# Laying small vectors, the router and the spatial weights out by channel on the host, in a hybrid decoder trunk

## The chip, the cores and the metric

The kernel runs on one core of a Trainium2 chip. The metric is the device time of one execution in microseconds; the host's preparation of the inputs is not in it. A core has a matrix engine (TensorE, PE in the profile), a vector engine (VectorE, DVE), an activation engine (ScalarE, ACT), a general one (GpSimd, POOL) and an engine that mostly issues transfers (SyncE, SP). Data lie in SBUF (128 partitions) and in PSUM, where the matmuls write. SP and ACT each issue transfers on a queue of their own: q1 (SP) and q10 (ACT) in the profile.

## The reference

x is 256 tokens by 1024 channels in float32. There are two layers, each a mixer and a feed-forward block, and a final RMS norm. What the change touches is in the mixer:

```
h = RMSNorm(x; norm_mix);  a, gate, u, v = split(h @ W_in, 4)       # 512 columns each
c = a * sigmoid(gate)
c = silu(group_norm(causal_depthwise_conv(c, conv_w, width 31) + conv_b; conv_ng, conv_nb))
u = gelu(u);  v = head_norm(gelu(v); sgu_ng, sgu_nb)                # 4 heads of 128 columns
ws = tril(sgu_w)                                                    # 4 heads, 128 x 128
g = u * (ws @ v + sgu_b)                                            # per chunk of 128 tokens
x = x + concat(c, g) @ W_out
x = x + FFN(RMSNorm(x; norm_ffn))       # layer 0: dense SwiGLU; layer 1: top 2 of 8 experts
```

## The kernel before

The program runs mixer 0, the dense block, mixer 1, the experts and the final norm one after the other, with one stream of weights under all of them. The weights lie in DRAM as blocks of up to 1 MB; `load_raw` (L325 to L344) issues one on SP into one of 11 raw buffers (`wraw`). A unit of 128 x 1024 is split for the exact three-pass float32 matmul: its high part `whi` by ACT (L353), its low part `wlo` by DVE or POOL (L358). A buffer comes free when its splits are done, or, where the weights are used unsplit, its matmuls.

A mixer (`mixer`, L557) is written as a list of operations for a small scheduler. Each operation is added by `add(engine, cost, function, reads, writes, delay)`; the scheduler sorts the whole list by modelled costs, by the length of the path behind an operation and by the delay after which its result counts as ready (2.0 us for SP's small loads, 4.0 for ACT's), and issues the program in that order. Each engine then runs its own instructions in that order, and an instruction that waits holds up all that are behind it on its engine.

In mixer 0, x comes in two halves (`xs`). ACT squares it (L706) for the RMS norm and, with DVE, makes the two parts `xh` (L699) and `xl` (L701) of each 128 channels out of PE's transposes (L686), scaled with a gain from `vt`. The conv gate and value (`gate`, `a`) come out of PSUM through DVE (L808, L812), which multiplies them by the token's 1/rms; the GLU product is L818, and the depthwise conv is one DVE instruction per tap (L863, L865), some taps on POOL (L842) and PE (L854). u and v are projected next; v's statistics are L933 to L935, its normalisation L941 on ACT, its gain and offset (`sgb`) L947 on DVE and POOL, the product with the spatial weights (`wst`) L954 on PE, and the gate L958. The output projection is L997.

The small inputs: `vt` (128 x 64) holds the per-channel vectors, a column each for 128 channels, and `cwt` (128 x 2 x 124) the conv taps. Both are made on the chip. Seven small loads bring rows (`rowa`, `crow`, `rowb`), PE transposes them (L744, L762, L764), and DVE and ACT copy them out (L745, L766, L768). `wst` is loaded by ACT with `sgu_w` as it is, four rows of 512 bytes for each partition (L771), transposed by PE (L927) and multiplied by the triangle `trim` out of PSUM (L929). `sgb` is two loads on ACT's queue (L774) that put one row of 2 KB into each of 128 partitions. The router (`rw`) is loaded in the dense block.

Of the kernel before, what the change touches and what calls it, by code (L numbers as in the profile page):

```python
# [7 lines left out]
F32 = mybir.dt.float32  # L8
# [3 lines left out]
AF = mybir.ActivationFunctionType  # L12
OP = mybir.AluOpType
# [3 lines left out]
P = 128  # L17
# [3 lines left out]
KD = D // P  # L21
C = 512
NC4 = C // P
W = 31
# [3 lines left out]
E = 8  # L28
# [36 lines left out]
class Schedule:  # L65
# [12 lines left out]
    def add(self, eng, cost, fn, r=(), w=(), table=None, delay=None):  # L78
        i = len(self.ops)
        deps = set()  # L80
        for b in r:
            if b in self.writer:
                deps.add(self.writer[b])
        for b in w:
            if b in self.writer:
                deps.add(self.writer[b])
            deps.update(self.readers.get(b, ()))
        for b in r:
            self.readers.setdefault(b, []).append(i)
# [150 lines left out]
    return loads, units, plan, rest  # L240


LOADS = 35


# [35 lines left out]
def hybrid_trunk(  # L281
    ctx: ExitStack,
    tc: tile.TileContext,
    x, norm_mix, conv_w, conv_b, conv_ng, conv_nb, sgu_ng, sgu_nb, sgu_w, sgu_b, norm_ffn, moe_router, norm_final, blocks,
    out,
):
    nc = tc.nc
    V = nc.vector
    A = nc.scalar
    G = nc.gpsimd  # L290
    T = nc.tensor
# [16 lines left out]
    loads, units, plan, rest = weight_plan()  # L308
# [135 lines left out]
    ident = consts.tile([P, P], F32, name="ident")  # L444
# [6 lines left out]
    trim = mixc.tile([P, P], F32, name="trim")  # L451
# [10 lines left out]
    vt = mixl.tile([P, 64], F32, name="vt")  # L462
    cwt = mixc.tile([P, 2, W * NC4], F32, name="cwt")
# [93 lines left out]
    def mixer(l, sg, nxt, rt=None):  # L557
        with ExitStack() as c2:
# [3 lines left out]
            add = S_.add  # L562
# [161 lines left out]
            if l == 0:  # L724
                add("ACT", 0.1, lambda: A.activation(va4[:, 0, 0:1], mhalf[:, 0:1], AF.Sigmoid), w=(("va4", 0),), table="sigmoid")
                e_warm(WARM[0], 3)
                sg.begin()
                xt = sg.t
                r = sg.r
                rowa = pool.tile([16, P], F32, name="rowa")  # L730
                rowb = pool.tile([48, P], F32, name="rowb")
                crow = pool.tile([W * NC4, 2, P], F32, name="crow")

                def small_load(dst, src, nm):
                    add("SP", 0.1, lambda: nc.sync.dma_start(dst, src), w=(nm, "loads"), delay=2.0)
# [12 lines left out]
                small_load(crow, conv_w.rearrange("l w o (k p) -> (w o k) l p", p=P), "crow")  # L748
                for i, g in enumerate((norm_ffn, conv_b, conv_ng, conv_nb, sgu_b)):
                    n0 = 0 if i == 0 else 8 + 8 * i  # L750
                    small_load(rowb[n0:n0 + (16 if i == 0 else 8)],
                               g.rearrange("l h t -> (l h) t") if i == 4 else g.rearrange("l (k p) -> (l k) p", p=P), ("rowb", i))
# [5 lines left out]
            if l == 0:  # L758
                ps, nm = new_tr()

                def tc_(ps=ps):
                    T.transpose(ps[:, :48], rowb, ident[:48, :48])  # L762
                    for l_ in range(2):
                        T.transpose(ps[:, 128 + 128 * l_:128 + 128 * l_ + W * NC4], crow[:, l_], ident[:W * NC4, :W * NC4])  # L764
                add("PE", 0.33, tc_, r=["crow"] + [("rowb", i) for i in range(5)], w=(nm,))
                add("ACT", 0.25, lambda ps=ps: A.activation(vt[:, 16:], ps[:, :48], AF.Copy), r=(nm,), w=("vt1",))  # L766
                for l_ in range(2):
                    add("ACT", 0.28, lambda ps=ps, l_=l_: A.activation(  # L768
                        cwt[:, l_], ps[:, 128 + 128 * l_:128 + 128 * l_ + W * NC4], AF.Copy), r=(nm,), w=(("cwt", l_),))

            add("ACT", 0.1, lambda: nc.scalar.dma_start(wst, sgu_w[l].rearrange("h t s -> t h s")), w=("wst",), delay=4.0)  # L771
            def e_gains():
                for i, g in enumerate((sgu_ng, sgu_nb)):
                    add("ACT", 0.1, lambda i=i, g=g: nc.scalar.dma_start(  # L774
                        sgb[:, i], bass.AP(tensor=g.tensor, offset=g.offset + l * C, ap=[[0, P], [1, C]])),
                        w=[("sgb", i)] + [("sig", i, j) for j in range(2) if rt], delay=4.0)

            if not rt:
# [141 lines left out]
                        r=("yfree",), w=(("grow", h),), delay=4.0)  # L920


            ps, nm = new_tr()
# [685 lines left out]
    with tc.manual_schedule():  # L1609
# [12 lines left out]
        moe(stages[3], rt)  # L1622


_INS = ["x", "norm_mix", "conv_w", "conv_b", "conv_ng", "conv_nb", "sgu_ng", "sgu_nb", "sgu_w", "sgu_b", "norm_ffn", "moe_router",
        "norm_final", "blocks"]
_OUTS = [((1, S, D), "float32")]


# [19 lines left out]
```

## Time and profile before

| what | value |
|---|---|
| runs | 1062.58, 1065.30, 1065.91 us; median 1065.3 |
| the profiled execution | 1065.07 us; its span 1063.3 us |
| mean granted clock of TensorE | 0.981 |
| PE busy | 1023.6 us (96% of the span) |
| DVE, ACT, POOL busy | 323.6, 260.0, 145.3 us |
| DMA | 343.57 MB, mean 323 GB/s |

The span runs from the first to the last instruction, and every time in the rows counts from its start. What the profiled execution takes beyond its span (1.77 us) lies before and after it. Averages over the span hide that the stages differ, so the rows further down are taken by stage.

### The profile page before, as it was taken

To read this page: it belongs to the slowest core of one execution; us is meant where nothing else is said; L and a number is where in the kernel's file an instruction comes from. 1 tells how busy PE (TensorE), PEld (TensorE's weight loads), DVE (VectorE), ACT (ScalarE), POOL (GpSimd) and SP (SyncE) were. 2 spreads that over 40 slices of the span, in tenths; PEclk is the share of its full clock that TensorE was granted. 3 is DMA by queue.
4 is the path that set the end of the run, shared out by engine and by line. 5 is a ranking of instruction groups with operands and counts; after the bars stand their busy time and mean duration, and the time that the engine had idled before them with its cause. 6 is when DMAs were issued, how large, how long until landed. Compare 5 with 4: busy or idle time off the path is not lost.

```text
span 1063.3 us, 30670 instructions
## 1 busy us (share of the span) xinstructions
PE 1023.6 (96%) x13824; PEld 731.3 (69%) x13824; DVE 323.6 (30%) x676; ACT 260.0 (24%) x442; POOL 145.3 (14%) x144
## 2 busy tenths in 40 slices
PE   7989999999999999999999999999999999999994
PEld 6967788888888685666666666666666666656662
DVE  4995655554469833001011001011001011001002
ACT  5585444453376630000000000000000000000002
POOL 2975000000069740000000000000000000000001
PEclk8999999999999978999999999999999999999998
DMA  8934554545566339999999999999999999999981
GB/s 280 422 125 169 189 190 167 198 161 195 198 242 223 139 121 397 418 420 415 419 418 417 418 419 417 417 418 417 400 419 417 414 418 419 386 419 418 409 332 47
DMA packets 54279, 343.57 MB, mean 323 GB/s; under 512 B 6852, under 2 KB 8700, under 8 KB 19836
## 3 DMA queue, kind: packets, MB, share of 16 engines
q1 hardware_dynamic: 51180, 339.40, 79.5%
q10 hardware_dynamic: 2960, 2.13, 0.8%
q8 instruction: 110, 1.80, 0.7%
q14 instruction: 29, 0.24, 0.1%
HBM read 340.46 MB, written 1.05 MB: 321 GB/s over the span
## 4 chain that ended last, share of the span: by engine, by line
PE 79%; DMA 13%; DVE 4%; ACT 2%; POOL 1%; issue 1%; POOLq 0%; SPq 0%; ACTq 0%; DVEq 0%
PE pg L1326 15%; PE mpd L1326 15%; PE pu L1326 15%; DMA wraw<-in_blocks_dram 11%; PE pd L414 6%; PE mm L997 4%; PE pu L381 2%; PE pg L382 2%; PE pg L383 2%; PE pg L381 2%; PE pu L383 2%; PE pu L382 2%; DVE acc L865 2%; PE ptr L1307 2%; PE pcomb L1421 2%; DMA crow<-in_conv_w_dram 1%
## 5 line engine op out<-in xcount | busy, mean ns | idle before, releaser
L1326 PE MATMUL pu<-wraw,xg 128*32 128x256 f32 (+1 forms) x3840 | 196.3, 362 | 1.9 <-DMA wraw<-in_blocks_dram 1.5
L1326 PE MATMUL pg<-wraw,xg 128*32 128x256 f32 (+1 forms) x3840 | 197.2, 364 | 0.4 <-DMA wraw<-in_blocks_dram 0.4
L1326 PE MATMUL mpd<-wraw,ah 128*32 128x256 f32 x3520 | 195.4, 380 | 2.0 <-DMA wraw<-in_blocks_dram 1.1
L1326 PEld LDWEIGHTS pu<-wraw,xg 128*32 128x32 f32 x3840 | 125.0, 110 | 68.8 <-DMA wraw<-in_blocks_dram 3.6
L1326 PEld LDWEIGHTS pg<-wraw,xg 128*32 128x32 f32 x3840 | 123.4, 111 | 67.7 <-issue 3.0
L1326 PEld LDWEIGHTS mpd<-wraw,ah 128*32 128x32 f32 x3520 | 112.4, 110 | 79.1 <-DMA wraw<-in_blocks_dram 2.6
L353 ACT ACTIVATE whi<-wraw 128x1024 fp32r<-128x1024 f32 x110 | 116.4, 1059 | 117.8 <-PE pd L414 31.1
L1352 DVE TENSOR_TENSOR sg<-sg,pu 128x512 f32<-128x512 f32 (+3 forms) x36 | 19.2, 559 | 399.8 <-PE pu L1326 341.8
L358 DVE TENSOR_TENSOR wlo<-wraw,whi 128x1024 fp32r<-128x1024 f32 x73 | 89.4, 1224 | 85.1 <-ACT whi L353 83.5
L1506 POOL TENSOR_TENSOR wraw<-xs,wraw 128x512 f32<-128x512 f32 (+1 forms) x4 | 3.9, 997 | 657.6 <-DVE xs L1426 657.6
L358 POOL TENSOR_TENSOR wlo<-wraw,whi 128x1024 fp32r<-128x1024 f32 x37 | 89.2, 2428 | 14.4 <-ACT whi L353 13.4
L865 DVE SCALAR_TENSOR_TENSOR acc<-big,cwt,acc 128x256 f32<-128x256 f32 x199 | 86.7, 479 | 1.7
L1351 ACT ACTIVATE sg<-pg 128x512 f32<-128x512 f32 (+3 forms) x36 | 16.5, 495 | 187.7 <-PE pg L1326 187.7
L1315 ACT ACTIVATE ah<-ptr 128x512 f32<-128x512 f32 (+2 forms) x24 | 13.0, 543 | 180.6 <-PE ptr L1364 105.2
L1313 DVE COPY ah<-ptr 128x256 f32<-128x256 f32 (+2 forms) x16 | 6.0, 374 | 128.9 <-PE ptr L1376 76.0
L798 PE MATMUL mm<-xh,whi 128*128 128x256 f32 x128 | 37.7, 294 | 3.7 <-ACT whi L353 3.7
L1315 ACT ACTIVATE xg<-ptr 128x320 f32<-128x320 f32 (+1 forms) x16 | 6.6, 410 | 129.1 <-PE ptr L1307 129.1
L800 PE MATMUL mm<-xh,wlo 128*128 128x256 f32 x128 | 36.7, 287 | 0.5 <-DVE wlo L358 0.5
L799 PE MATMUL mm<-xl,whi 128*128 128x256 f32 x128 | 36.6, 286 | 0.0
L381 PE MATMUL pu<-whi,xh 128*128 128x512 f32 (+1 forms) x96 | 36.5, 381 | 0.0
L381 PE MATMUL pg<-whi,xh 128*128 128x512 f32 (+1 forms) x96 | 36.2, 377 | 0.0
L382 PE MATMUL pg<-wlo,xh 128*128 128x512 f32 (+1 forms) x96 | 36.1, 376 | 0.0
(244 smaller groups left out, 1191.5 us busy)
## 6 DMA issues: line engine op xcount, KB each, us to landing
wraw<-in_blocks_dram SPq DMA_DIRECT2D x268, 1024.0 KB, 18.8
wraw<-in_blocks_dram SPq DMA_DIRECT2D x64, 768.0 KB, 17.4
wraw<-in_blocks_dram SPq DMA_DIRECT2D x10, 512.0 KB, 10.8
xs<-in_x_dram SPq DMA_DIRECT2D x2, 512.0 KB, 8.1
wst<-in_sgu_w_dram ACTq DMA_DIRECT2D x2, 256.0 KB, 16.1
grow<-in_norm_ffn_dram ACTq DMA_DIRECT2D x2, 256.0 KB, 3.7
wraw<-in_norm_final_dram SPq DMA_DIRECT2D x1, 512.0 KB
out_dram<-wraw SPq DMA_DIRECT2D x4, 128.0 KB, 2.5
```

The source lines that it names most:

```text
L353: A.activation(ready[i][0][:, :w], src, AF.Copy)
L358: eng.tensor_sub(ready[i][1][:, :w], src, ready[i][0][:, :w].bitcast(F32))
L381: T.matmul(bank, xs_[0][:, c, sl], w, start=first, stop=False)
L382: T.matmul(bank, xs_[0][:, c, sl], lo, start=False, stop=False)
L383: T.matmul(bank, xs_[1][:, c, sl], w, start=False, stop=last)
L414: T.matmul(b, s[:, k0 + j, sl], w[:, ws], start=(first and j == 0 and pi == 0), stop=(last and j == len(ids) - 1 and pi == 2))
L798: T.matmul(o, hi[:, ws], xt[0][:, k], start=(k == 0), stop=False)
L799: T.matmul(o, hi[:, ws], xt[1][:, k], start=False, stop=False)
L800: T.matmul(o, lo[:, ws], xt[0][:, k], start=False, stop=(k == KD - 1))
L865: V.scalar_tensor_tensor(accp, src, wv, accp if w else pa, op0=OP.mult, op1=OP.add)
L997: T.matmul(mm[ob[t][h]], a[:, ts], b[:, o + h * 512:o + h * 512 + 512], start=first and j == 0, stop=last and j == len(seq) - 1)
L1326: T.matmul(region(banks, w, g, q), x_(g, q), srcs[q], start=first and g % (512 // w) == 0, stop=last, skip_group_check=True)
```

## The change

The host lays out three new inputs in place of eight. `vectors` (128 x 312) has the 64 columns of `vt` and behind them the 248 of `cwt`; two loads on SP fill the tiles directly, the first behind the first half of x, the second behind the loads of the first `a` unit. `router` has the layout of its tile. `sgu_wt` has the spatial weights with the source position on the partitions, 2 KB in each. The transposes and their copies are gone, and the product with the triangle reads `wst` in SBUF. In mixer 0 the loads of `sgb` and `wst` on ACT's queue now depend on the last `xh` (`later_`).

```diff
+def small_blocks(inputs):
+    rows = [inputs[nm].reshape(-1, P) for nm in ("norm_mix", "norm_ffn", "conv_b", "conv_ng", "conv_nb", "sgu_b", "conv_w")]
+    return dict(vectors=np.concatenate(rows).T, router=inputs["moe_router"][0].reshape(KD, P, E).transpose(1, 0, 2).reshape(P, KD * E),
+                sgu_wt=inputs["sgu_w"].transpose(0, 3, 1, 2).reshape(2, P, 4 * P))
...
                     if h == 0:
-                        small_load(rowa, norm_mix.rearrange("l (k p) -> (l k) p", p=P), "rowa")
+                        small_load(vt, vectors[:, :64], ("vt0", "vt1"))
                         want(plan[0, "gate0"][0])
-                ps, nm = new_tr()
-                add("PE", 0.11, lambda ps=ps: T.transpose(ps[:, :16], rowa, ident[:16, :16]), r=("rowa",), w=(nm,))
-                add("DVE", 0.1, lambda ps=ps: V.tensor_copy(vt[:, :16], ps[:, :16]), r=(nm,), w=("vt0",))
                 e_quad(sg, 0)
                 want(plan[0, "a0"][0])
-                small_load(crow, conv_w.rearrange("l w o (k p) -> (w o k) l p", p=P), "crow")
-                for i, g in enumerate((norm_ffn, conv_b, conv_ng, conv_nb, sgu_b)):
...
+                small_load(cwt.rearrange("p l c -> p (l c)"), vectors[:, 64:], [("cwt", l_) for l_ in range(2)])
...
-            add("ACT", 0.1, lambda: nc.scalar.dma_start(wst, sgu_w[l].rearrange("h t s -> t h s")), w=("wst",), delay=4.0)
+            later_ = [("xh", KD - 1)] if l == 0 else []
+            add("ACT", 0.1, lambda: nc.scalar.dma_start(wst.rearrange("p h t -> p (h t)"), sgu_wt[l]), r=later_, w=("wst",), delay=4.0)
...
-                        sgb[:, i], bass.AP(tensor=g.tensor, offset=g.offset + l * C, ap=[[0, P], [1, C]])),
+                        sgb[:, i], bass.AP(tensor=g.tensor, offset=g.offset + l * C, ap=[[0, P], [1, C]])), r=later_,
...
-            def tw(ps=ps):
-                for h in range(4):
-                    T.transpose(ps[:, h * P:(h + 1) * P], wst[:, h], ident)
-            add("PE", 0.44, tw, r=("wst",), w=(nm,))
-            add("DVE", 0.6, lambda ps=ps: V.tensor_tensor(wst, ps.rearrange("p (h t) -> p h t", h=4),
-                                                          trim[:, None, :].to_broadcast([P, 4, P]), op=OP.mult), r=(nm,), w=("wst",))
+            add("DVE", 0.6, lambda: V.tensor_tensor(wst, wst, trim[:, None, :].to_broadcast([P, 4, P]), op=OP.mult), w=("wst",))
...
-            nc.scalar.dma_start(rw, moe_router[0].rearrange("(k p) e -> p k e", p=P))
+            nc.scalar.dma_start(rw.rearrange("p k e -> p (k e)"), router)
```

The scheduler orders the changed list anew, so more moves than the diff says. SP's row before, at the start of mixer 0 (`wraw` are the weight loads):

```order
1 L738 DMA xs<-in_x_dram 128x2x512
2 L735 DMA rowa<-in_norm_mix_dram 16x128
3 L344 DMA wraw<-in_blocks_dram 128x1024
4 L738 DMA xs<-in_x_dram 128x2x512
5 L344 DMA wraw<-in_blocks_dram 128x1024
6 L735 DMA crow<-in_conv_w_dram 124x2x128
7 L735 DMA rowb<-in_norm_ffn_dram 16x128
8 L735 DMA rowb<-in_conv_b_dram 8x128
9 L735 DMA rowb<-in_conv_ng_dram 8x128
10 L735 DMA rowb<-in_conv_nb_dram 8x128
11 L735 DMA rowb<-in_sgu_b_dram 8x128
12 L344 DMA wraw<-in_blocks_dram 128x1024 x2
```

And SP's row in the changed kernel, from its start:

```order
1 L742 DMA xs<-in_x_dram 128x2x512
2 L739 DMA vt<-in_vectors_dram 128x64
3 L352 DMA wraw<-in_blocks_dram 128x1024
4 L742 DMA xs<-in_x_dram 128x2x512
5 L352 DMA wraw<-in_blocks_dram 128x1024
6 L739 DMA cwt<-in_vectors_dram 128x248
7 L352 DMA wraw<-in_blocks_dram 128x1024 x2
8 L352 DMA wraw<-in_blocks_dram 128x2048 x75
```

Six small loads between the second and the third weight load have become one. On ACT the three loads of its own queue were at the start before (the activations are squares into `mm_140`, gatings into `xh`, splits into `whi`):

```order
1 L774 DMA sgb<-in_sgu_ng_dram 128x512
2 L725 ACT_TABLE_LOAD
3 L725 ACTIVATE va_125<-mhalf 128x1
4 L774 DMA sgb<-in_sgu_nb_dram 128x512
5 L771 DMA wst<-in_sgu_w_dram 128x4x128
6 L706 ACTIVATE mm_140,ms<-xs 128x512 x2
```

In the changed kernel the same place of mixer 0 ends ACT's first gatings like this:

```order
10 L714 ACTIVATE mm_140,ms<-xs 128x512
11 L361 ACTIVATE whi<-wraw 128x1024
12 L707 ACTIVATE xh_146<-tr_144,vt 128x256
13 L361 ACTIVATE whi<-wraw 128x1024
14 L707 ACTIVATE xh_146<-tr_144,vt 128x256
15 L361 ACTIVATE whi<-wraw 128x1024
16 L714 ACTIVATE mm_140,ms<-xs 128x512
17 L760 DMA sgb<-in_sgu_ng_dram 128x512
18 L760 DMA sgb<-in_sgu_nb_dram 128x512
19 L756 DMA wst<-in_sgu_wt_dram 128x512
```

The three loads stand behind all gatings, all four squares and four splits. On DVE, in mixer 0, before, from the first conv gate on (`big<-mm,rr` drains a PSUM bank, `big_117<-big_117` is the GLU product, `acc` are taps; the product of `wst` with the triangle stands at row 93, behind v's statistics):

```order
14 L808 TENSOR_TENSOR big_117<-mm_137,rr 128x256
15 L812 TENSOR_TENSOR big_117<-mm_138,rr 128x256
16 L818 TENSOR_TENSOR big_117<-big_117 128x256
17 L808 TENSOR_TENSOR big_117<-mm_139,rr 128x256
18 L863 TENSOR_SCALAR acc_141<-big_117,cwt 128x256
19 L865 SCALAR_TENSOR_TENSOR acc_141<-big_117,cwt,acc_141 128x256 x4
```

The same place of DVE in the changed kernel:

```order
15 L794 TENSOR_TENSOR big_117<-mm_137,rr 128x256
16 L798 TENSOR_TENSOR big_117<-mm_138,rr 128x256
17 L794 TENSOR_TENSOR big_117<-mm_139,rr 128x256
18 L909 TENSOR_TENSOR wst<-wst,trim 128x512
19 L804 TENSOR_TENSOR big_117<-big_117 128x256
20 L849 TENSOR_SCALAR acc_141<-big_117,cwt 128x256
21 L851 SCALAR_TENSOR_TENSOR acc_141<-big_117,cwt,acc_141 128x256 x2
```

The product of `wst` with the triangle has moved from row 93 to row 18, ahead of the first GLU product. In mixer 1 it stands at row 181, behind the first two taps, where before it stood at row 258, behind v's statistics.

## Rows read from the trace of the kernel before

**Rows 1.** Windows by stage: us; PE, PEld, DVE, ACT, POOL busy; PEclk; DMA share; GB/s.

```profile
0.00:108.70 108.70, 94.47 (x510) 78.94 (x511) 80.05 (x182) 70.26 (x133) 67.68 (x61) 0.94 0.66 251
108.70:294.00 185.30, 185.30 (x873) 153.40 (x873) 96.57 (x94) 80.92 (x89) 0.56 (x1) 1.00 0.50 182
294.00:393.30 99.30, 95.24 (x552) 80.94 (x550) 73.48 (x196) 64.27 (x120) 72.14 (x77) 0.97 0.48 174
393.30:1063.30 670.00, 648.57 (x11892) 418.04 (x11892) 73.54 (x207) 44.52 (x101) 4.90 (x6) 0.98 0.97 396
```

**Rows 2.** Waits of SP's queue, 290 to 425: total us, times, longest us.

```profile
SPq L344 <- PE mm L1081: 18.0, 1, 18.0
```

**Rows 3.** Timeline of SP, 0 to 16: start, us, instruction.

```profile
0.82 0.45 SPq L738 DMA_DIRECT2D xs<-in_x_dram  x1
...
12.75 3.25 SPq L344 DMA_DIRECT2D wraw<-in_blocks_dram  x3
```

**Rows 4.** Waits of ACT, 0 to 24.

```profile
ACT whi L353 <- DMA wraw<-in_blocks_dram: 5.1, 4, 2.5
```

**Rows 5.** Timeline of PE, 10 to 13; in brackets the idle before.

```profile
12.02 0.58 PE L798 MATMUL mm<-xh,whi 128*128 128x256 f32 x1 [3.67 <-ACT whi L353]
```

**Rows 6.** Timeline of DVE, 18 to 27.

```profile
24.77 1.54 DVE L818 TENSOR_TENSOR big<-big 128x256 f32<-128x256 f32 x1
```

**Rows 7.** Windows of mixer 0, columns as in Rows 1.

```profile
12.00:18.60 6.60, 6.11 (x26) 5.71 (x27) 4.61 (x9) 5.95 (x13) 0.71 (x1) 0.50 0.76 203
...
24.00:58.00 34.00, 31.97 (x205) 28.40 (x203) 33.32 (x68) 21.66 (x37) 32.10 (x19) 1.00 1.01 421
```

**Rows 8.** Timeline of DVE, 60 to 75.

```profile
67.51 0.25 DVE L938 SCALAR_TENSOR_TENSOR nb<-mv,rv 128x8 f32<-128x8 f32 x1
...
72.98 1.00 DVE L947 TENSOR_TENSOR big<-big,sgb 128x512 f32<-128x512 f32 x1 [0.55 <-ACT big L941]
```

**Rows 9.** Timeline of ACT, 64 to 73.

```profile
67.97 1.28 ACT L895 ACT_TABLE_LOAD   x1
```

**Rows 10.** Groups of ACT by line, 0 to 24: count, busy us, mean ns, idle.

```profile
L353 ACT ACTIVATE whi<-wraw 128x1024 fp32r<-128x1024 f32 x5 | 5.3, 1056 | 5.1 <-DMA wraw<-in_blocks_dram 5.1
L699 ACT ACTIVATE xh<-tr,vt 128x256 fp32r<-128x256 f32 x8 | 3.4, 462 | 0.2 <-PE tr L686 0.2
L706 ACT ACTIVATE mm<-xs 128x512 f32<-128x512 f32 x4 | 2.4, 603 | 3.9 <-DMA xs<-in_x_dram 3.8
```

**Rows 11.** The page's DMA issues: count, KB each, us to landing.

```profile
wst<-in_sgu_w_dram ACTq DMA_DIRECT2D x2, 256.0 KB, 16.1
grow<-in_norm_ffn_dram ACTq DMA_DIRECT2D x2, 256.0 KB, 3.7
```

**Rows 12.** DMA queues, 308.5 to 309: packets, MB, share.

```profile
q10 hardware_dynamic: 1, 0.00, 0.3%
```

**Rows 13.** Timeline of ACT, 304 to 307.

```profile
305.32 0.37 ACTq L771 DMA_DIRECT2D wst<-in_sgu_w_dram  x1
```

**Rows 14.** DMA queues, 309 to 315.

```profile
q1 hardware_dynamic: 314, 2.31, 92.3%
q10 hardware_dynamic: 309, 0.16, 9.0%
```

**Rows 15.** DMA queues, 318 to 322, where `sgb` with rows of 2 KB follows.

```profile
q10 hardware_dynamic: 143, 0.25, 27.7%
```

**Rows 16.** Timeline of DVE in mixer 1, 304 to 312 and 338 to 356.

```profile
309.68 2.06 DVE L865 SCALAR_TENSOR_TENSOR acc<-big,cwt,acc 128x256 f32<-128x256 f32 x4
...
350.63 0.69 DVE L929 TENSOR_TENSOR wst<-tr,trim 128x512 f32<-128x512 f32 x1 [0.39 <-PE tr L927]
...
351.62 1.56 DVE L947 TENSOR_TENSOR big<-big,big 128x512 f32<-128x512 f32 x1
```

**Rows 17.** Groups of DVE by line and form, 23.8 to 61.1.

```profile
L865 DVE SCALAR_TENSOR_TENSOR acc<-big,cwt,acc 128x256 f32<-128x256 f32 x61 | 26.2, 479 | 0.5
L818 DVE TENSOR_TENSOR big<-big 128x256 f32<-128x256 f32 x3 | 5.4, 1794 | 0.1
```

More of the change, by code (lines that the diff above doesn't have):

```diff
@@ L240, in weight_plan @@
     return loads, units, plan, rest
+def small_blocks(inputs):
+    import numpy as np
+    rows = [inputs[nm].reshape(-1, P) for nm in ("norm_mix", "norm_ffn", "conv_b", "conv_ng", "conv_nb", "sgu_b", "conv_w")]
+    return dict(vectors=np.concatenate(rows).T, router=inputs["moe_router"][0].reshape(KD, P, E).transpose(1, 0, 2).reshape(P, KD * E),
+                sgu_wt=inputs["sgu_w"].transpose(0, 3, 1, 2).reshape(2, P, 4 * P))
 LOADS = 35
@@ L283, in hybrid_trunk @@
     tc: tile.TileContext,
-    x, norm_mix, conv_w, conv_b, conv_ng, conv_nb, sgu_ng, sgu_nb, sgu_w, sgu_b, norm_ffn, moe_router, norm_final, blocks,
+    x, vectors, router, sgu_ng, sgu_nb, sgu_wt, norm_ffn, norm_final, blocks,
     out,
@@ L729, in mixer @@
                 r = sg.r
-                rowa = pool.tile([16, P], F32, name="rowa")
-                rowb = pool.tile([48, P], F32, name="rowb")
-                crow = pool.tile([W * NC4, 2, P], F32, name="crow")
                 def small_load(dst, src, nm):
-                    add("SP", 0.1, lambda: nc.sync.dma_start(dst, src), w=(nm, "loads"), delay=2.0)
+                    add("SP", 0.1, lambda: nc.sync.dma_start(dst, src), w=(*nm, "loads"), delay=2.0)
                 for h in range(2):
@@ L740, in mixer @@
                     if h == 0:
-                        small_load(rowa, norm_mix.rearrange("l (k p) -> (l k) p", p=P), "rowa")
+                        small_load(vt, vectors[:, :64], ("vt0", "vt1"))
                         want(plan[0, "gate0"][0])
-                ps, nm = new_tr()
-                add("PE", 0.11, lambda ps=ps: T.transpose(ps[:, :16], rowa, ident[:16, :16]), r=("rowa",), w=(nm,))
-                add("DVE", 0.1, lambda ps=ps: V.tensor_copy(vt[:, :16], ps[:, :16]), r=(nm,), w=("vt0",))
                 e_quad(sg, 0)
                 want(plan[0, "a0"][0])
-                small_load(crow, conv_w.rearrange("l w o (k p) -> (w o k) l p", p=P), "crow")
-                for i, g in enumerate((norm_ffn, conv_b, conv_ng, conv_nb, sgu_b)):
-                    n0 = 0 if i == 0 else 8 + 8 * i
-                    small_load(rowb[n0:n0 + (16 if i == 0 else 8)],
-                               g.rearrange("l h t -> (l h) t") if i == 4 else g.rearrange("l (k p) -> (l k) p", p=P), ("rowb", i))
+                small_load(cwt.rearrange("p l c -> p (l c)"), vectors[:, 64:], [("cwt", l_) for l_ in range(2)])
             e_quad(sg, 1)
@@ L757, in mixer @@
             e_rstd(sg)
[L758 to L769, printed above, removed]
-            add("ACT", 0.1, lambda: nc.scalar.dma_start(wst, sgu_w[l].rearrange("h t s -> t h s")), w=("wst",), delay=4.0)
+            later_ = [("xh", KD - 1)] if l == 0 else []
+            add("ACT", 0.1, lambda: nc.scalar.dma_start(wst.rearrange("p h t -> p (h t)"), sgu_wt[l]), r=later_, w=("wst",), delay=4.0)
             def e_gains():
@@ L920, in mixer @@
                         r=("yfree",), w=(("grow", h),), delay=4.0)
-            ps, nm = new_tr()
-            def tw(ps=ps):
-                for h in range(4):
-                    T.transpose(ps[:, h * P:(h + 1) * P], wst[:, h], ident)
-            add("PE", 0.44, tw, r=("wst",), w=(nm,))
-            add("DVE", 0.6, lambda ps=ps: V.tensor_tensor(wst, ps.rearrange("p (h t) -> p h t", h=4),
-                                                          trim[:, None, :].to_broadcast([P, 4, P]), op=OP.mult), r=(nm,), w=("wst",))
+            add("DVE", 0.6, lambda: V.tensor_tensor(wst, wst, trim[:, None, :].to_broadcast([P, 4, P]), op=OP.mult), w=("wst",))
             for i in range(8):
@@ L1622, in hybrid_trunk @@
         moe(stages[3], rt)
-_INS = ["x", "norm_mix", "conv_w", "conv_b", "conv_ng", "conv_nb", "sgu_ng", "sgu_nb", "sgu_w", "sgu_b", "norm_ffn", "moe_router",
-        "norm_final", "blocks"]
+_INS = ["x", "vectors", "router", "sgu_ng", "sgu_nb", "sgu_wt", "norm_ffn", "norm_final", "blocks"]
 _OUTS = [((1, S, D), "float32")]
@@ L1637 @@
     inputs["blocks"] = weight_blocks(inputs)
+    inputs.update(small_blocks(inputs))
     arrays, args = {}, []
```

## The prediction

> **What bounds the kernel now.** I read the stages first. The span falls into mixer 0 (to 108.7 us), the dense block (to 294), mixer 1 (to 393.3) and the experts [rows 1]. TensorE is busy for 185.30 of 185.3 us in the dense block and 648.57 of 670 in the experts, where the weight stream also fills 0.97 of the DMA engines. Neither stage has slack to take up a delay or to give away a gain. In mixer 1 the weight loads already wait 18.0 us for a buffer that a matmul must free [rows 2]: they run as far ahead as the buffers let them, so an earlier mixer doesn't start the experts with more weights. I therefore carry any shift of a mixer's end to the end of the span, one for one. The change touches only the mixers, where PE has 14.2 and 4.1 us of gaps. That is where the sum is made.
>
> In mixer 0 the issues show that SP sent the first half of x at 0.82 and then stood in its small loads; the weight loads behind a0 went out only at 12.75 [rows 3]. ScalarE's first splits of the weights waited 5.1 us for raw weights [rows 4], and the first gate matmul started at 12.02, after 3.67 us idle [rows 5]. VectorE reached the first GLU product at 24.77 [rows 6]. From 24 to 58 VectorE is busy for 33.32 of 34 us (conv taps), beside 31.97 of PE and a full DMA [rows 7]: after the first GLU product, VectorE's order decides when the spatial product of mixer 0 can start. A start that is later by one microsecond there is later by one at the end.
>
> **What the change removes.** Seven small loads become two, one of them behind the first half of x and one behind a0; the transposes of the vectors, their four copies out of PSUM and the four transposes of the spatial weights per mixer go. None of these stood where an engine was waited for, except that the small loads held SP. So the copies are worth nothing beside the stream of [rows 7], and the loads are worth an earlier start. An idle queue landed 256 KB in 3.7 us [rows 11]. I put x's first half at 0.82 + 3.7 = 4.5 us, the first gate block behind it (0.6 MB with the vectors, at the 421 GB/s of [rows 7]) at 5.9, and with one split (1.06) and one gating (0.46) of [rows 10] the first gate matmul at 7.5, 4.5 us sooner. Before, the first GLU product came 12.75 us after that matmul [rows 5, 6], so VectorE would be there at about 20.3, and at 20.7 with the third PSUM drain that now stands ahead of it. Bounds: the gain at the start is 0 if x and its gate block land no sooner, 4.5 if all does.
>
> **What it moves.** In VectorE's row order of the changed kernel the masking product of the spatial weights (`wst<-wst,trim`) no longer stands behind the statistics of v, but ahead of the first GLU product and so of every conv tap; in mixer 1 it stands behind the first two taps. It waits for the load of `wst`, whose issue has moved too: in mixer 0 it now stands in ScalarE's row behind four squares, eight gatings, four splits and the two loads of `sgb`, where before it was issued near the start of the program. Nothing on VectorE can pass the product: the GLU product, all taps and the drains of the PSUM banks are queued behind it, and PE waits for those banks.
>
> When does `wst` land in mixer 0? ScalarE begins with x at 4.5 and has four squares of 0.60 with a read of about 0.15 beside, eight gatings at 0.40 (their 0.46 overlap) and four splits at 0.96 (1.06, overlapping): 3.0 + 3.2 + 3.8 = 10.0 us [rows 10], so the `sgb` issues come at 14.5. In mixer 1 the load of `wst` was issued at 305.32 [rows 13], but its first packet shows only at about 308.7 [rows 12]: 3.4 us. From then on its packets go about one for one with those of the weight stream, 309 against 314 in 6 us [rows 14], or 51 per us; with rows of 2 KB, as now, 143 in 4 us or 36 per us [rows 15]. I take 42, which is a pair of 8 + 2 KB at the 421 GB/s of [rows 7] and lies between. The three loads are 384 rows of 2 KB in one queue, so 9.1 us (7.5 to 10.7). `wst` lands at 14.5 + 3.4 + 9.1 = 27.0 (25.4 to 28.6), and VectorE, there at 20.7, waits 6.3 us. The whole gain of the earlier start goes into that wait.
>
> The profile calls one 2-KB row a packet, and the queues alternate by it. The Trainium skill (page "DMA: Bandwidth & Descriptors", section "Queues, rings and completion order") has each engine drain a whole packet of some 9 to 17 descriptors from one queue before it goes to the next. By that the small rows would pass many at a time; [rows 14] don't bear it out. It is the second rival below.
>
> The product itself took 0.69 us from PSUM [rows 16]. Now both its inputs are in SBUF, with POOL busy for 32.10 of 34 us [rows 7]. The nearest rows: the same shape out of SBUF took 1.00 and 1.56 [rows 8, 16]; the GLU product, half as wide and in the same stretch, took 1.79 on average [rows 17], which for twice the width is 3.6 at most. I take 1.5, near the row of the same shape; ends 0.69 and 3.6. The Trainium skill speaks against the change here (page "SBUF — State Buffer", section "Who interferes with whom"): a VectorE instruction with two SBUF inputs and a GpSimd instruction that reads SBUF exclude each other for a whole instruction. The GLU product's 1.79 against a tap's 0.48 at the same width agrees; by the rule the upper price would hold, and the sum below would be 1073.8, where the lower end gives 1068.0.
>
> Mixer 0: first GLU product at 27.0 + 1.5 = 28.5 against 24.77, so +3.7. Later a little comes back. Before, ScalarE loaded the silu table at 67.97 ahead of the normalisation of v [rows 9], though its input was there at 67.76; VectorE's gain product then started at 72.98 and waited 0.55 us for it [rows 8]. Now the normalisation precedes the table, and VectorE's own row (eight taps of 0.48 [rows 17] and two short ones, 4.4 us behind that input) sets the start, at 72.2 on the old scale: -0.8. Mixer 0 ends 2.9 us later.
>
> Mixer 1: the queue of ScalarE is idle there and the issue isn't moved. With 128 rows instead of 512, `wst` lands at 305.32 + 3.4 + 128/42 = 311.8, sooner than the 16.1 us of before [rows 11]. VectorE gets to the product after its first tap of the row at 309.68 [rows 16], at 310.2: 1.6 us of wait, and 1.5 for the product. One more tap stands ahead of the statistics (+0.5), one tap and one product of that width fewer between these and the variance (-0.9), and the old product with its idle 0.39 goes (-1.1, [rows 16]). Sum +1.6.
>
> **Sum.** 1065.07 (the profiled execution, span 1063.3 and 1.77 around it) + 2.9 + 1.6 = 1069.6 us, so 1069.5. The profiled execution lies 0.2 below the median of 1065.3. The contiguous load of the router, the removed PE work in mixer 1 and the 2-KB rows of `wst` cost and give nothing else: the router lands a whole dense block before its use.
>
> **Rivals.**
> First: the wait eats the gain and no more. If ScalarE gets through a little sooner (13.8) and the rows pass at 51 per us, `wst` is in at 13.8 + 3.4 + 7.5 = 24.7 and, with a product of 0.69, the GLU product comes at 25.4: +0.6 - 0.8. In mixer 1 it is 311.2, +1.0 + 0.7 + 0.5 - 0.9 - 1.1. Both sum to 0: 1065 us. For it: all three values lie inside the rows' bounds. Against: they must all fall to one side.
>
> Second, and on the other side: the small rows pass in bunches, or the weight stream has gaps when they come. Then 0.79 MB need only 1.9 us at 421 GB/s, `wst` is in at 14.5 + 3.4 + 1.9 = 19.8 before VectorE is there, and the first GLU product stands at 20.7 + 1.5 = 22.2, 2.6 sooner; with -0.8, mixer 0 gains 3.4. In mixer 1 it lands at 309.3, there is no wait, and 1.5 + 0.5 - 0.9 - 1.1 is nothing. That gives 1061.6 us. It decides from a landing below some 21 us. For it: with SP free from the start, loads could stop early for lack of buffers. Against: [rows 14], and the DMA share in [rows 7].
>
> Third: the wait costs the clock as well. From 12 to 18.6 the granted clock was 0.50 (the 1.2 GHz level) with PE nearly always busy, after PE had idled [rows 5, 7]. If PE, without banks for over 4 us, falls to that level again for 6.6 us, 3.3 us more are lost: 1073 us.
>
> **How the numbers follow.** The forecast has 0.50, the first rival 0.26, the second 0.19, the third 0.05. The measurement can tell about 0.3%, 3.2 us, from no change: over 1068.5 is slower, under 1062.1 faster. Of the forecast some 0.07 lies under 1068.5 (a product near 0.69 together with an early landing); of the first rival 0.03 lies in faster. Faster then is 0.21, same 0.30, slower 0.49. The forecast's own range is 1066.5 to 1073.5; the second rival takes the low end to 1061.
>
> **What would show it.** In the changed profile: the first gate matmul near 7.5; the `wst` load issued near 15 and landed near 27; VectorE idle for about 6 us before `wst<-wst,trim`, released by the DMA; the first GLU product at 28 or later, and PE waiting for drains in between; in mixer 1 a wait of 1 to 2 us on the same load. Wrong if VectorE has no wait on `wst` in mixer 0, or if the product lands at 0.7 us and its load below 24; wrong in my carrying of shifts if mixer 0 ends earlier or later and the experts don't follow.

## The result and the profile after

The changed kernel takes 1072.5 us (median of five, 1070.62 to 1074.95) against 1065.54 before (1062.58 to 1065.91). The ratio is 1.0069, with a 95% interval of 1.0053 to 1.0086: slower by some 7 us. The forecast said slower, 1069.5, with a range of its own from 1066.5 to 1073.5. The sign was right, and so was the cause in mixer 0, VectorE's wait at the masking product. The size was not: about 4.5 us were expected, and most of the loss came in mixer 1, where 1.6 were.

First, where it lies. I take the first matmul of the dense block and the first of the experts as borders, in each run's own profile:

| profile | dense block begins | to the experts | experts to end of span | span |
|---|---|---|---|---|
| before | 107.75 | 285.52 | 670.0 | 1063.3 |
| after | 110.16 | 291.46 | 669.2 | 1070.8 |
| difference | +2.4 | +5.9 | -0.8 | +7.5 |

The experts take what they took to within 0.8 us, so a shift of mixer 1's end passes to the end of the span [rows 1], as assumed. Mixer 0 costs 2.4 us (forecast 2.9), the stretch with mixer 1 in it 5.9 (forecast 1.6). Each row is one execution: eleven of the profiles below are of programs that are the same up to the first gate matmul, and they have it at 8.56 to 10.51. So 1 or 2 us between two profiles at the first border need not be the edit's. I follow the load of `wst` first. In the timeline of ACT of the changed kernel, the three late loads are issued:

```profile
13.18 0.38 ACTq L760 DMA_DIRECT2D sgb<-in_sgu_ng_dram  x1
13.59 0.45 ACTq L760 DMA_DIRECT2D sgb<-in_sgu_nb_dram  x1
...
14.08 0.45 ACTq L756 DMA_DIRECT2D wst<-in_sgu_wt_dram  x1
```

They share the engines with the weight stream from 17 to 28 like this (view of the DMA queues: packets, MB, share):

```profile
q1 hardware_dynamic: 515, 3.79, 83.3%
q10 hardware_dynamic: 417, 0.76, 18.2%
```

Where both have work, they alternate nearly one packet of 2 KB for one of 8 KB: from 17 to 22 q10 has 47, 37, 56, 40 and 42 in each microsecond, and q1 43, 42, 55, 40 and 43. That is near the 42 that I had taken from [rows 14, 15]. VectorE then stands at the masking product (timeline of DVE):

```profile
21.79 0.42 DVE L794 TENSOR_TENSOR big<-mm,rr 128x256 f32<-128x256 f32 x1 [0.17 <-PE mm L786]
28.28 1.53 DVE L909 TENSOR_TENSOR wst<-wst,trim 128x512 f32<-128x512 f32 x1 [6.07 <-DMA wst<-in_sgu_wt_dram]
29.73 0.41 DVE L804 TENSOR_TENSOR big<-big 128x256 f32<-128x256 f32 x1
```

The wait is 6.07 us (forecast 6.3), the product 1.53, and the first GLU product stands at 29.73 instead of 24.77 [rows 6]. The same in mixer 1, where the wait is 3.90 and the product 2.64:

```profile
318.02 2.64 DVE L909 TENSOR_TENSOR wst<-wst,trim 128x512 f32<-128x512 f32 x1 [3.90 <-DMA wst<-in_sgu_wt_dram]
```

Both durations follow POOL. Its timeline has a low-part split under way each time, two of them from 24.50 and three from 313.00:

```profile
24.50 4.76 POOL L366 TENSOR_TENSOR wlo<-wraw,whi 128x1024 fp32r<-128x1024 f32 x2
...
313.00 7.11 POOL L366 TENSOR_TENSOR wlo<-wraw,whi 128x1024 fp32r<-128x1024 f32 x3 [0.32 <-ACT whi L361]
```

POOL ends at 29.26 and 320.11; VectorE's product ends at 29.81 and 320.66, each time 0.55 us later. By these ends it did not run slowly, but stood until POOL's instruction was done.

The clock is the third thing. Where PE idled 3.52 us ahead of the spatial product of mixer 0, its granted clock fell to 0.50, the lower level of 1.2 GHz, for a part of these windows (columns as in Rows 1); I call that a dip:

```profile
72.00:78.40 6.40, 2.99 (x17) 2.88 (x18) 6.04 (x15) 5.86 (x8) 6.32 (x5) 0.85 0.00 0
78.40:88.00 9.60, 9.15 (x29) 4.70 (x29) 8.71 (x22) 3.98 (x7) 5.99 (x3) 0.92 0.56 196
300.00:306.00 6.00, 5.02 (x28) 4.83 (x29) 3.47 (x10) 5.51 (x14) 3.50 (x4) 0.72 0.15 33
```

The kernel before has 1.00 in 72 to 88, and from 290 to past 370. Here PE's first 16 spatial matmuls take 3.15 us and not 2.05, and the head of mixer 1 (last row) loses 1.55 us up to the first drain.

### The profile page after: what moved, and what is told of

The parts are those of the page before. It is cut to its first block, busy times and chain, and to the rows that moved or that the text cites. A ratio compares the mean times of both kernels' runs of the same rounds, so it can differ in the third digit from the quotient of the medians.

```text
span 1070.8 us, 30631 instructions
## 1 busy us (share of the span) xinstructions
PE 1026.7 (96%) x13812; PEld 735.1 (69%) x13812; DVE 322.0 (30%) x675; ACT 258.9 (24%) x439; POOL 144.2 (13%) x144
## 4 chain that ended last, share of the span: by engine, by line
PE 76%; DMA 12%; DVE 7%; ACT 2%; POOL 1%; issue 1%; SPq 0%; POOLq 0%; ACTq 0%; DVEq 0%
PE pg L1305 16%; PE pu L1305 15%; PE mpd L1305 15%; DMA wraw<-in_blocks_dram 9%; PE pd L422 5%; DVE acc L851 5%; PE mm L976 4%; DMA wst<-in_sgu_wt_dram 2%; PE pg L390 2%; PE pu L389 2%; PE pg L389 2%; PE pu L390 2%; PE pu L391 2%; PE pg L391 2%; PE ptr L1286 2%; PE pcomb L1400 2%
## 5 line engine op out<-in xcount | busy, mean ns | idle before, releaser
L1305 PEld LDWEIGHTS mpd<-wraw,ah 128*32 128x32 f32 x3520 | 115.8, 110 | 76.0 <-issue 2.7
```

Source lines behind the costliest of these rows:

```text
L1305: T.matmul(region(banks, w, g, q), x_(g, q), srcs[q], start=first and g % (512 // w) == 0, stop=last, skip_group_check=True)
```

## The experiments

The theories: A, the time goes into VectorE's waits at the masking product, which its new place in the row brings; B, the late loads take the queues from the weight stream; C, PE's gaps cost it the clock. Ratios below are to the kernel before, with their intervals.

**e1: the product behind the variance of v, in both mixers**

```diff
-            add("DVE", 0.6, lambda: V.tensor_tensor(wst, wst, trim...), w=("wst",))
...
             e_rsqrt(rv, va, 8, ("vva",), ("rv",))
+            add("DVE", 0.6, lambda: V.tensor_tensor(wst, wst, trim...), r=("vva",), w=("wst",))
```

> The changed kernel, with the masking product of the spatial weights made to follow the variance of v in both mixers, as its place was before the change. Theory A (the 7 us come from VectorE standing at that product for a load that lands late): no wait on wst in either mixer, first GLU product near 21.5 instead of 29.7, mixer 0 some 3 to 4 us sooner than before the change, mixer 1 as before: 1061 to 1062.5 us, ratio to before about 0.997. Theory B (the three late loads take the queues from the weight stream, and the stream bounds mixer 0 in any order): the first GLU product is early, but PE and the splits then wait for raw weights, and the time stays at 1064 to 1066. Theory C (the granted clock falls when PE starts and stops in another rhythm, the product's place matters little): 1069 or more.

1064.66 us, 0.9997 (0.9982 to 1.0012). The place of the product alone is worth 7.8 us (1072.5 against 1064.66), more than the whole loss: A holds for that. This isn't quite its place of before, where it stood behind `nb`, the row that the normalisation waits for (67.51, the product at 69.77); here it stands between the variance and `nb`. What that costs is told under e9. But the 3 to 4 us below the kernel before did not come. The first GLU product is there at 20.89, and the dense block starts at 104.48, 3.3 sooner; of that 2.2 go again before the experts. B's mark, a time kept up by raw weights, isn't there: the dense block is early. The product took 0.68 us in mixer 0, out of SBUF as in the changed kernel, with no split on POOL. PE's timeline shows where some of the gain stayed:

```profile
68.79 3.75 PE L933 MATMUL mm<-big,wst 128*128 128x128 f32 x16 [2.96 <-ACT big L881]
72.33 2.97 PE L976 MATMUL mm<-wraw,big 128*128 128x512 f32 x4
```

The spatial product starts 6.9 us sooner than before, after 2.96 us of idle, and it and the first output matmuls run for the most part at a clock of 0.50.

**e2: the same in mixer 0 only**

```diff
+            if l:
+                add("DVE", 0.6, ... masking product as in the changed kernel ...)
...
+            if l == 0:
+                add("DVE", 0.6, ... behind the variance of v ...)
```

> The changed kernel, with the masking product behind the variance of v in mixer 0 only; in mixer 1 it stays behind the first two taps. Theory A: mixer 0 gains as in the run with both moved, mixer 1 loses what it lost in the changed kernel (3.9 us of wait and a product of 2.6, some 4.4 us at the experts' start): 1065.5 to 1067, about 4.5 above the run with both moved. Theory B: the difference is the same, but both lie 3 us higher. Theory C: no difference between the two.

1067.13 us, 1.0016 (0.9998 to 1.0034). Just above A's range. So of the 7.8 us, 5.4 are the place in mixer 0 and 2.5 that in mixer 1 (expected 4.5). The product of mixer 1 again ended 0.55 after POOL's split, which ran 306.80 to 313.91:

```profile
311.57 2.89 DVE L910 TENSOR_TENSOR wst<-wst,trim 128x512 f32<-128x512 f32 x1 [3.64 <-DMA wst<-in_sgu_wt_dram]
```

**e3 and e4: the three loads at the start again** (e3 with the product in the changed kernel's rule, e4 with it late)

```diff
-            later_ = [("xh", KD - 1)] if l == 0 else []
+            later_ = []
```

> The changed kernel without the condition on the last xh: in mixer 0 the loads of sgb and wst go out at the start of the program again, as before, and the masking product moves to the head of VectorE's row, ahead of the first xl. Theory A: wst lands near 7 us, VectorE waits there until then and holds up xl, the first gate matmul comes 1 to 2 us later than in the changed kernel, but no wait stands ahead of the taps: first GLU product at 23 to 24, mixer 0 ends 1 to 3 us sooner than before the change, mixer 1 loses its 4.4: 1066.5 to 1069. Theory B: the loads no longer disturb the stream between 16 and 28, so this gains most of the runs that keep the mixer 1 order: under 1066. Theory C: 1070 or more.

1069.88 us, 1.0030 (1.0013 to 1.0048): between A's range and C's 1070, so the time decides neither. Of A's marks, VectorE's wait and a first GLU product near 24 are there, but mixer 0 ended only 0.2 us sooner than before the change, not 1 to 3. VectorE stood at the product until 9.21, ahead of the first `xl`; the first gate matmul came at 11.71, the GLU product at 24.11.

> Both edits: the loads of sgb and wst at the start of the program, the masking product behind the variance of v in both mixers. Against the run with the product late and the loads late this shows alone what the later place of the three loads is worth. Theory A: at the start they take 0.79 MB ahead of or beside x and the first weights, at most 1.9 us: 0 to 1.9 us slower than that run, 1061.5 to 1064. Theory B: faster than that run by 1 us or more, since the stream is left alone from 16 to 28. Theory C: no difference.

1066.97 us, 1.0016 (1.0001 to 1.0032): 2.3 us slower than e1. So issuing them late is right by itself, and B is refuted here: what the loads cost at the start (first gate matmul 11.38 instead of 8.96) is more than what they cost the stream later.

**e5, e6, e8: PE kept busy in its gaps** (24 matmuls of ones ahead of mixer 0's spatial product in e5; 12 more at the head of mixer 1 in e6; e8 is the changed kernel with both)

```diff
+            if not rt:
+                def fill():
+                    for _ in range(24):
+                        T.matmul(mm[0][:, :P], ones, ones, start=True, stop=True)
+                add("PE", 0.0, fill, r=[("v", t, h) for t in range(NT) for h in range(4)], w=(("mm", 0),))
```

> The run with the product late and the loads late (1064.7), plus 24 matmuls of ones by ones into a free PSUM bank on PE just ahead of the spatial product of mixer 0, where PE idled 2.96 us and the granted clock then fell to 0.50 from about 67 to 75.5 (spatial product 3.75 us and first output matmuls 2.97 instead of 2.05 and 1.88). Their results are overwritten. Theory C (the start's gain was lost to the clock): the clock stays at 1.00 there, spatial to first output matmul 2 us instead of 3.5, dense block some 2 to 3.5 us earlier: 1061 to 1062.7. Theory D (the output projection then waits for the conv channels and PE's speed there is covered): spans of spatial and output matmuls shrink, the dense block starts at the same time: 1064 to 1065.

1065.38 us, 0.9995 (0.9980 to 1.0011): nothing gained. The clock did stay at 1.00 from 56 to 112, and the spatial product led to the output matmuls in 1.79 us instead of 3.54. But I had mis-sized the filling:

```profile
67.50 5.60 PE L926 MATMUL mm<-ones 128*128 128x128 f32 x48
72.94 1.95 PE L938 MATMUL mm<-big,wst 128*128 128x128 f32 x16
```

(The trace has two rows for each of these matmuls.) The filling took 5.4 us where the gap was 3, and the spatial product came 15.46 us behind the first statistics instead of 13.13.

> The run before this one plus 12 such matmuls at the head of mixer 1, where PE idles 1.4 us for the residual sum and the clock then fell in three of four profiles with a dip of 1.6 us. Theory C: the first drain of mixer 1 comes 1.5 us earlier relative to the dense block's start: 1059.5 to 1061.5. Theory D: no change to the run before, as mixer 1's head waits for 1/rms anyway: equal within 0.5 us.

1069.01 us, 1.0029 (1.0015 to 1.0043): slower. The 12 matmuls waited themselves 1.99 us for the residual sum, then took 4.27 us: they came behind the gap and not in it. The clock fell at that head all the same, so this says nothing on C.

> The changed kernel itself with both groups of filling matmuls, product early. Its profile had three dips of the clock that the kernel before did not have (78 to 82, 302 to 306, 342 to 346), some 1.6 us each. Theory A and C together (of the 7 us about 4 are the waits, about 3 the clock): the first two dips go, 1068.5 to 1070. Theory A alone (dips fall in covered time): 1071.5 to 1073.

1071.57 us, 1.0052 (1.0034 to 1.0071): not told apart from the changed kernel. As both fillings were misplaced, this is inconclusive.

**e7: spatial weights transposed on the chip as before the change, all else changed**

```diff
-            add("ACT", 0.1, lambda: nc.scalar.dma_start(wst.rearrange("p h t -> p (h t)"), sgu_wt[l]), r=later_, w=("wst",), delay=4.0)
+            add("ACT", 0.1, lambda: nc.scalar.dma_start(wst, sgu_w[l].rearrange("h t s -> t h s")), r=later_, w=("wst",), delay=4.0)
...
+            add("PE", 0.44, tw, r=("wst",), w=(nm,))
+            add("DVE", 0.6, lambda ps=ps: V.tensor_tensor(wst, ps..., trim...), r=(nm,), w=("wst",))
-            add("DVE", 0.6, lambda: V.tensor_tensor(wst, wst, trim...), w=("wst",))
```

> The changed kernel with the spatial weights loaded and transposed as before the change (four rows of 512 bytes, PE transposes, product out of PSUM behind the variance of v), all else as changed: vectors by two loads, the three loads of ScalarE's queue late. Theory A (the harm of the change is the product's place alone): like the run with the product late, 1064 to 1065.5; the load of 512 small rows lands later in both mixers but ahead of its use. Rival: the transposes on the chip are worth something by themselves, and this is 1 us or more slower than that run.

1059.79 us, 0.9943 (0.9923 to 0.9963): 6 us faster than the kernel before, and 4.9 faster than e1. Neither theory had that. PE's timeline of mixer 0 has the transposes between the last matmuls of u, and the spatial product in two halves:

```profile
64.31 0.60 PE L913 MATMUL tr<-ident,wst 128*128 128x128 f32 x4
...
69.08 1.06 PE L940 MATMUL mm<-big,wst 128*128 128x128 f32 x8
72.05 1.16 PE L940 MATMUL mm<-big,wst 128*128 128x128 f32 x8 [1.92 <-DVE big L933]
```

PE's idle is in pieces of 1.15 and 1.92 us here, and the clock holds 1.00 from 62 on, through the output projection. The stretch from the dense block's start to the experts takes 285.54, to 0.02 us what it took before the change.

**e9: these transposes in mixer 0 only**

```diff
+            if l == 0:
+                ... load, transposes and product of e7 ...
+            else:
+                ... load and late product of e1 ...
```

> Mixer 0 with the spatial weights as before the change (loaded in rows of 512 bytes, transposed by PE, product out of PSUM), mixer 1 with the host's layout and the product behind the variance of v. The run with the transposes in both mixers took 1059.8, the one without any 1064.7. Theory E (the transposes break up the wait of PE ahead of the spatial product, and the clock stays up where the output projection follows; this is mixer 0's): most of the 4.9 us come back, 1060 to 1061.5, the dense block starts at 103 to 103.5. Theory F (the difference lies in mixer 1, in the dip of the clock at its head and the product's 1.2 us): 1063 to 1064.5.

1062.69 us, 0.9976 (0.9963 to 0.9989): in the middle. By the medians 2.0 of the 4.9 us would be mixer 0's and 2.9 mixer 1's, so neither E nor F alone. But the profile does not show mixer 0's part, and E's marks failed in it. The dense block starts at 105.08 and not at 103 to 103.5, and from the first gate matmul to the dense block e9 takes 95.53 us, just as e1 does. The clock fell at the output projection although the spatial product is in halves here too, after 2.14 us of idle where e7 had 1.92 (first two rows e9, last row e7):

```profile
72.23 1.16 PE L946 MATMUL mm<-big,wst 128*128 128x128 f32 x8 [2.14 <-DVE big L939]
73.22 5.29 PE L989 MATMUL mm<-wraw,big 128*128 128x512 f32 x8
...
73.04 3.60 PE L983 MATMUL mm<-wraw,big 128*128 128x512 f32 x8
```

What e9's profile gains on e1's, 1.5 us, is a dip at the head of mixer 1 that e1 has and e9 has not. In mixer 1 the masking product takes 1.20 us in e1 and 1.21 in e9, ending 0.55 us behind a short POOL sum. It stands ahead of `nb`, which comes 3.80 us behind the variance in e1; in e7 and before the change `nb` comes first, 2.79 and 2.78 us behind the variance (first two rows e1, last two e7):

```profile
342.89 1.20 DVE L916 TENSOR_TENSOR wst<-wst,trim 128x512 f32<-128x512 f32 x1
346.17 0.16 DVE L917 SCALAR_TENSOR_TENSOR nb<-mv,rv 128x8 f32<-128x8 f32 x1
...
342.98 0.16 DVE L924 SCALAR_TENSOR_TENSOR nb<-mv,rv 128x8 f32<-128x8 f32 x1
346.08 0.69 DVE L915 TENSOR_TENSOR wst<-tr,trim 128x512 f32<-128x512 f32 x1 [0.39 <-PE tr L913]
```

From the variance to the spatial product mixer 1 takes 9.48 and 9.51 us in e1 and e9, and 8.28 in e7 and before. PE's wait ahead of its first half in e1 is part of that; e7 has none there:

```profile
351.85 1.16 PE L933 MATMUL mm<-big,wst 128*128 128x128 f32 x8 [2.56 <-POOL big L926]
```

So 1.2 us of e7's lead are the place that I gave the product in e1. No run has the host's layout with the product behind `nb`.

**e11: ten filling matmuls in place of 24**

```diff
-                    for _ in range(24):
+                    for _ in range(10):
```

> The run with the product late and the loads late, with 10 matmuls of ones ahead of the spatial product of mixer 0. The 24 of the earlier run took 5.4 us and reached past the wait of 2.96 us, so the spatial product started 3 us late; ten are 2.3 us. Theory C, right-sized: the clock stays at 1.00 from 66 to 76, spatial product to first output matmul 1.8 to 2 us instead of 3.5, dense block at 102 to 103 instead of 104.5: 1062.5 to 1063.5. Rival: the clock falls somewhere else instead, or the projection waits for the conv channels: 1064 to 1065.5.

1063.89 us, 0.9986 (0.9970 to 1.0002). In the profiled execution it does what C says (no dip from 56 to 112 or from 290 to 380, dense block at 101.66, 2.8 us ahead of e1):

```profile
65.43 2.48 PE L926 MATMUL mm<-ones 128*128 128x128 f32 x20
68.49 2.29 PE L938 MATMUL mm<-big,wst 128*128 128x128 f32 x16 [0.58 <-DVE big L931]
70.61 1.88 PE L981 MATMUL mm<-wraw,big 128*128 128x512 f32 x4
```

But the runs spread from 1059.46 to 1065.80, and the median isn't told apart from e1's. The granted clocks of the single runs go with this spread: 0.986 and 0.987 in the three below 1061.5, 0.982 and 0.983 in the seven above 1063.5; e1's twelve have 0.980 to 0.984. So the filling seems to hold the clock in some executions and not in others. Where the others dip isn't on record. C is shown for this place in one profile, the second fastest of twelve; as a gain in time it isn't shown.

**e12: e7 with the three loads some 30 us later still** (`later_` on the last conv input, the loads added behind the gates)

> The best version so far (vectors by two loads, spatial weights transposed on the chip, 1059.8), with the three loads of mixer 0 on ScalarE's queue later still, behind the first half of v, some 20 us later. Theory B (they take the queues from the weight stream between 16 and 28, when mixer 0 is short of weights): 1058 to 1059.3. Rival (the stream has buffers ahead by then): 1059.5 to 1060.3.

1059.55 us, 0.9949 (0.9930 to 0.9967): as e7. With the loads at 45.92 and later, the stream moved 10.46 MB from 20 to 45 instead of 9.86, and nothing came of it that six runs can tell (e7: 0.9923 to 0.9963). That is the rival to B.

**e13: the changed kernel with `wst` first of the three loads**

```diff
-            add("ACT", 0.1, ... sgu_wt[l]), r=later_, w=("wst",), delay=4.0)
+            add("ACT", 0.1, ... sgu_wt[l]), r=later_, w=("wst", "wst_load"), delay=4.0)
...
-                        sgb[:, i], bass.AP(...)), r=later_,
+                        sgb[:, i], bass.AP(...)), r=[*later_, "wst_load"],
```

> The changed kernel with one thing moved: of the three late loads of ScalarE's queue, wst goes first and the two of sgb behind it. The scheduler then puts the masking product three rows further ahead, before the first drains. Theory A with its model of the landing (issue near 13.2, 3.3 us to the first packet, 128 rows at 40 per us, 1.5 us for the last ones): lands at 21.2, VectorE hardly waits beyond what the drains wait for 1/rms anyway, first GLU product at 23 to 24 instead of 29.7; mixer 1 as in the changed kernel: 1066.5 to 1069. Rival (the landing is set by something else than what stands ahead in the queue): lands at 26 or later, 1071 to 1073.

1067.28 us, 1.0021 (1.0004 to 1.0037): 5.2 us back, in A's range. Issued at 12.95, `wst` lands at 21.6 (model 21.2):

```profile
21.62 1.96 DVE L909 TENSOR_TENSOR wst<-wst,trim 128x512 f32<-128x512 f32 x1 [5.03 <-DMA wst<-in_sgu_wt_dram]
...
24.51 0.41 DVE L804 TENSOR_TENSOR big<-big 128x256 f32<-128x256 f32 x1
```

The two loads of 256 rows ahead of it in the queue were what made it late in mixer 0, as the count of packets said. Not all of the 5.2 us need be theirs. Of the 7.2 us between this profile and that of the changed kernel, 3.8 lie ahead of the dense block and 3.1 in the stretch with mixer 1, where `wst` is alone in its queue in both. There it landed 7.6 us after its issue instead of 8.7, and the product took 1.40 us instead of 2.64, again ending 0.55 behind a split. Whether that comes from the edit or from chance isn't shown.

## Why the prediction came out as it did

**The start** was mis-sized: the first gate matmul came at 9.82, 2.2 us sooner and not 4.5, as PE waited 3.30 us ahead of it until the low part of the weights was done (1.22 us on VectorE), which I had left out. It cost nothing, since all of it went into the wait.

**Landing, mixer 0**: 28.3 against 27.0. The first of the three was issued 1.3 us sooner (13.18 and not 14.5: ACT issued them while the last gating, split and square, which stand ahead of them in its row, were still to run, to 15.7). The first packet shows 3.5 us after it (forecast 3.4), and the rate was right (45 packets a microsecond from 17 to 26, 42 taken). Left out was the tail: q10 has its last full microsecond at 25 to 26, ten more packets come up to 28, and VectorE starts 2.3 us after that microsecond. In mixer 1 it is the same term: packets from 312.7 to 316.2, start at 318.0, so 8.7 us from issue and not 6.5. The whole-packet turns of the Trainium skill (page "DMA: Bandwidth & Descriptors", section "Queues, rings and completion order"), my second rival, show in none of these counts.

**The product's price** of 1.5 was right in mixer 0 (1.53) and wrong in mixer 1 (2.64). The Trainium skill (page "SBUF — State Buffer", section "Who interferes with whom") has a VectorE instruction with two SBUF inputs and a GpSimd instruction that reads SBUF exclude each other for a whole instruction. The trace agrees where POOL ran splits: eight products in the profiles of after, e2, e3, e8 and e13 end 0.55 us behind one of them. It doesn't where POOL ran a power operation on a few columns (e1, mixer 0); beside that the same product takes 0.68. So the price was never a width times a rate, but what is left of POOL's 2.4 us, and 0.55. I had weighed the rule and then taken the row of the same shape.

**Between GLU and spatial product in mixer 0**, two errors that cancel. Ahead by 5.0 us of delay, VectorE made up 3.6 until the statistics (62.37 against 61.01), most of it because two of the three GLU products (0.41 and 0.42 us) ran beside an idle POOL (it waited 5.9 us for ACT, which waited for VectorE):

```profile
L804 DVE TENSOR_TENSOR big<-big 128x256 f32<-128x256 f32 x3 | 2.4, 798 | 0.0
```

That is 0.8 us on average against 1.79 [rows 17], 3.0 in all. The normalisation ahead of the table, and VectorE's row without the old product (0.69, behind 0.33 of wait), gave 1.7 more (forecast 0.8), so the spatial product even started 0.3 sooner than before. From there to the dense block 2.7 were lost (34.75 against 32.04), some 1.6 to 1.9 of it to the clock, going by e5 and e11, which take 32.85 and 33.17 without a dip; the rest isn't traced. So that 2.4 came near 2.9 was in part luck.

**The step that failed is the +1.6 of mixer 1**; it measured +5.9. By terms: the head's clock cost 1.55 (not in the sum); wait, product and extra tap 4.9 up to the statistics (forecast 3.6). They are 3.90, 2.64 and 0.5 by themselves, 2.1 of which VectorE made up by then; the landing and POOL's split are what the forecast had too short. From there to the spatial product nothing changed, where I had credited -2.0. The credit of 0.9 ahead of the variance came (3.18 us against 4.21), the other 1.1 didn't: VectorE's own `sgb` product waited 0.64 us for ACT, and what VectorE saved wasn't last. Later 0.6 came back.

**The third rival** (the clock) happened, but elsewhere than I put it: over 24 to 58 the clock is 0.95, with a dip whose cost isn't shown; on the path it fell at the gap ahead of the spatial product and at mixer 1's head. The dip at mixer 1's head came in six of the twelve profiles with the same 1.4-us gap (all but e6 and e8), whether the product stood early or late. What decides it stays open. Of the 3.9 us that e7's profile leads e1's, 1.3 lie ahead of the dense block, 2.2 in the stretch with mixer 1 (1.5 by that dip, 1.2 by the product ahead of `nb`, less 0.5 elsewhere) and 0.4 in the experts. That the transposes, or the halves of the spatial product, help by themselves is not shown: e9 has both in mixer 0, and its profile is no faster there than e1's.

**The carrying of shifts** held: the experts take 668.9 to 670.6 us in all fourteen profiles. But the row that I gave for it was misread. L1081 is a count matmul of the routing and reads no weights. That the loads run up to the buffers' limit shows in another row of the view of [rows 2]:

```profile
SPq L344 <- POOL wlo L358: 72.5, 11, 14.9
```

**What the change is worth.** Its start (vectors in two loads, late loads on the second queue) is a gain, and the host's layout of the spatial weights is the harm. e7, with the one and without the other, is the fastest version besides e12: 1059.8 against 1065.5. Between it and the changed kernel lie 12.7 us. 7.8 of them are the place in the order that the layout sets free (e1); the other 4.9 are accounted for only in part, as said above.

## What to carry to other kernels

A step that is taken out can have been what held another one back in an order made by costs: with the transposes gone, the product was ready by its modelled 4-us load and went to the head of an in-order engine, where the load really took 14.2 us from its issue to the product. Look at the row order after the change, and at each instruction that waits for a transfer ahead of a long queue; give such a load first place in its queue or tie its user to a later event. And price a VectorE instruction with two SBUF inputs by what runs on POOL beside it.

## What the runs showed of the hardware that I had not expected

A POOL power operation on a few columns (59.93 to 61.60 in e1) did not hold up the masking product (0.68 at 60.22), where the splits did, and a 256-wide sum too (in mixer 1 of e1 it ends at 343.54 and the product at 344.09). VectorE started 2.3 and 1.8 us after the bulk of the packets that it waited for, beside the weight stream, in the two mixers of the changed kernel. Work that PE is given in a gap can cost more than the gap: ten matmuls of ones by ones took 2.48 us, 24 took 5.60.
